# Regrouping the small matrix products of a gated linear recurrence: one visit across three heads, states and transposed outputs on their own

## The chip, the cores and the metric

The kernel runs on one core of one Trainium2 chip. Its engines work at the same time, each through its own instructions in order: TensorE (matrix products; PE in the profile, its weight loads PEld), VectorE (DVE), ScalarE (ACT), GpSimd (POOL), and SyncE (SP), which here only issues DMAs. TensorE writes its results to PSUM, eight banks of 128 x 512 floats; everything else lies in SBUF. The metric is device time of one execution in microseconds (us), the median of three.

## What is computed

One inference step of two layers over 272 prompt positions (16 learned ones ahead of 256) and 64 sample positions (8 sequences of 8), model width 2048. Layer 0 is a gated linear recurrence with 16 heads of 128, layer 1 a sliding-window attention. Only layer 0 is touched. For each head its projections are

```
q, fx, i, g = split(x @ w_in)            # four 128-wide columns per head
f = lb + (1 - lb) * sigmoid(fx);  k = 1 - f;  v = i
```

and in chunks of positions

```
b = cumsum(log f)
a[t, s] = sum_k q[t] * exp(b[t] - b[s]) * k[s]       # s <= t
o = (q * exp(b)) @ s0 + a @ v
s_new = exp(b_last) * s0 + (k * exp(b_last - b))^T @ v
```

After it, o is divided by its root mean square over the head, scaled, multiplied by silu(g), and goes through the output projection w_out, a residual and a LayerNorm. Outputs are the new states, the cache of layer 1 and the activations.

## The kernel before, in words

**Big products.** All projections run through `Stream`. A tile is one 128-wide output column block: 16 k blocks of 128, and for each k block three products of 128 x 128 weights with 128 x 336 activations (weights and activations are split in a high and a low part to keep float32 accuracy, L225 to L227). Weights come by DMA on SP into `raw` (L148), ACT casts the high part `whi` (L159), DVE subtracts to get `wlo` (L170), up to seven chunks of four k blocks ahead. A tile accumulates in a PSUM bank of the pool `pj` (three banks); at its end its `epi` function empties it. `kouter=True` runs several tiles side by side, chunk by chunk.

**Small work.** After the three products of each k block, `Stream.step` is called once. Generators in `st.side` hold everything else; a generator says by `yield n` that it wants its next piece n steps later, and at most two pieces run in a step. So the order on every engine is written out by these numbers, and no scheduler changes it. A piece issues its instructions at that place of all queues: its small products stand between two big ones on TensorE, its DVE work between two weight splits. A tile has 16 steps, a head's four tiles (in the order f, q, i, g) have 64.

**A head.** `epi_f` makes f and k on ACT and DVE. `epi_q` starts `head_chain`: three rounds of `update` (pairs, fours, eights) build scaled copies of k and q in `kx` and `qx` (a step of a tree of decay factors), then four `level` calls multiply them in 32-column products into the bank `lv_a` (52 steps into the head). `pick` copies the valid part by masks into `a32`; further updates (16, 32, 64) follow. When tile i is there, a second visit of TensorE makes the wide levels in `lv_b`, the outputs `po` of the head before, and the transposes `pk` and `pv`. From these the pieces `V`, `K`, `Ks`, `Vs` (ACT, DVE) and `vm` (POOL, L636) are made; `head_tail`, moved on by `adv`, multiplies the new states `psp` and `pss`, stores them, makes `po`, its squares and `ss` (L709 to L711), `osc` (L714), its transposes `pt` into the old `lv_b` bank (L720), and `og` with its split into `oh` and `ol`, the activations of the output projection.

So TensorE leaves the big products twice per head. The first visit, in tile g, holds levels 0 to 3 of head h, the states of h-1 and the transposes of `osc` of h-2. The second, at the start of the next head's tile f, holds the wide levels of h, the output of h-1, and `pk`, `pv` of h.

**End of the layer.** The output projection's tiles z0, z1, z2 run side by side, the rest one by one; `z_chain` takes each into a residual and running moments.

PSUM pools: `pj` three banks, `lv` two, `mm` three (all of `pk`, `pv`, `psp`, `pss`, `po`).

Of the kernel before, what the change touches and what calls it, by code (L numbers as in the profile page):

```python
# [21 lines left out]
F32 = mybir.dt.float32  # L22
# [217 lines left out]
def hybrid_trunk(tc, x_prompt, x_sample, state_hgrn, cache_k, cache_v, meta, w_in0, lb_logits, norm_w, w_out0,  # L240
# [7 lines left out]
    with es:  # L248
# [97 lines left out]
        for nm, w in (("f", 384), ("qp", 448), ("iT", 384), ("at", 3 * 132), ("a32", 96), ("sq0", 288),  # L346
                      ("sq1", 288), ("qi0", 177), ("qi1", 177), ("w64", 72)):
            one[nm] = hp1.tile([P, w], F32, tag=nm, name=nm)
            nc.gpsimd.memset(one[nm], 1.0 if nm == "w64" else 0.0)
        kx, qx = [], []  # L350
        for q in range(1, 4):
            for l, nm, w in ((kx, "kx", 384), (qx, "qx", 448)):
                l.append(hp1.tile([P, w], F32, tag=f"{nm}{q}", name=f"{nm}{q}"))
                nc.gpsimd.memset(l[-1], 0.0)
# [90 lines left out]
        def epi_g(h):  # L445
            def epi(ps):
                d = head_state(h)
                sg = hp.tile([P, T], F32, tag="sg", name=f"sg{h}")
                nc.scalar.activation(sg, ps, AF.Sigmoid)
                d["sg"] = sg  # L450
                s0 = hp.tile([P, 8, P], F32, tag="s0", name=f"s0_{h}")
                nc.sync.dma_start(s0, state_hgrn[0, :, h].rearrange("b k v -> k b v"))
                d["s0"] = s0

                def chain():
                    yield 2
                    nc.vector.tensor_tensor(sg, sg, ps, op=ALU.mult)  # L457
                    ready["g", h] = True
                st.spawn(chain())
            return epi  # L460
# [5 lines left out]
        def update(k, q, m, tot, n, k2=None, q2=None, nq=None):  # L466
# [5 lines left out]
            w = min(n, 448 - (m - 1)) // (2 * m) * 2 * m  # L472
# [4 lines left out]
            if q2 is not None and not nq:  # L477
                nc.scalar.copy(halves(q2, m - 1, m, w, True), halves(q, m - 1, m, w, True))
# [17 lines left out]
        tails = {}  # L496

        def adv(h):
            if h in tails:
                next(tails[h], None)  # L500

        def head_chain(h):
            d = head_state(h)
            kr, qp, a32, sq, qi = d["kr"], d["qp"], d["a32"], d["sq"], d["qi"]
            at = d["at"].rearrange("p (b w) -> p b w", b=3)
            kk = [kr] + kx
            qq = [qp] + qx

            def level(pl, o, li, wide=True):
                k, q = kk[min(li, 3)], qq[min(li, 3)]  # L510
                for blk in range(3):
                    for j in range(4 if blk < 2 else 3 if wide else 1):
                        c = blk * 128 + j * 32
                        nc.tensor.matmul(pl[32 * j:32 * j + 32, o + blk * 32:o + blk * 32 + 32], k[:, c:c + 32],
                                         q[:, c:c + 32], start=True, stop=True, tile_position=(0, 32 * j),
                                         skip_group_check=True)

            def pick(pl, o, li, wide=True):
                m0 = li * 96
                r = 96 if wide else 32  # L520
                nc.vector.copy_predicated(a32[:, 0:64], mk[:, m0:m0 + 64], pl[:, o:o + 64])
                nc.vector.copy_predicated(a32[0:r, 64:96], mk[0:r, m0 + 64:m0 + 96], pl[0:r, o + 64:o + 96])

            tot = {1: d["f"]}
            yield 3
            for li in range(3):
                m = 1 << li
                update(kk[li], qq[li], m, tot[m], 352, kk[li + 1], qq[li + 1])
                tot[2 * m] = total(h, m, tot[m], 352)
                yield 4  # L530

            k8, q8 = kk[3], qq[3]
            fs = hp.tile([P, 8], F32, tag="fs", name=f"fs{h}")
            t8 = tot[8]
            nc.gpsimd.tensor_copy(fs, t8[:, 36:44])
            w64 = d["w64"]
            nc.gpsimd.tensor_copy(w64[:, 0:64].rearrange("p (b t) -> p b t", t=8)[:, :, 7], fs)

            for s in range(3):
                n = 3 if s < 2 else 2  # L540
                nc.gpsimd.tensor_tensor(sq[:, 0:96 * n].rearrange("p (j w) -> p j w", w=96)[:, :, 40 * s:40 * s + 8],
                                        q8[:, 288:288 + 24 * n].rearrange("p (j w) -> p j w", w=24)[:, :, 8 * s:8 * s + 8],
                                        w64[:, 0:24 * n].rearrange("p (j w) -> p j w", w=24)[:, :, 8 * s:8 * s + 8],
                                        op=ALU.mult)
            yield 4

            pa = lv.tile([P, 512], F32, tag="lv", name=f"lv{h}_a")
            for li in range(4):
                level(pa, 96 * li, li)
            adv(h - 1)  # L550
            adv(h - 2)
            yield 1
            update(k8, q8, 8, t8, 272)
            tot[16] = hp.tile([P, 17], F32, tag="tot16", name=f"tot{h}_16")
            t8v = t8[:, 0:34].rearrange("p (b two) -> p b two", two=2)
            nc.vector.tensor_tensor(tot[16], t8v[:, :, 0], t8v[:, :, 1], op=ALU.mult)
            for li in range(4):
                pick(pa, 96 * li, li)
            adv(h - 1)
            yield 2  # L560
            t16 = tot[16][:, 16:17]
            update(k8, q8, 16, tot[16], 256, kk[1], qq[1])
            tot[32] = total(h, 16, tot[16], 256)
            nc.vector.tensor_scalar(qq[1][:, 271:272], q8[:, 271:272], t16, None, op0=ALU.mult)
            yield 3
            adv(h - 2)
            update(kk[1], qq[1], 32, tot[32], 256, kk[2], qq[2])
            nc.scalar.copy(qi[:, 144:161], qq[1][:, 255:272])
            t64 = total(h, 32, tot[32], 256)
            t128 = hp.tile([P, 2], F32, tag="t128", name=f"t128_{h}")  # L570
            nc.vector.tensor_tensor(t128[:, 0:1], t64[:, 2:3], t64[:, 3:4], op=ALU.mult)
            yield 3
            adv(h - 1)
            k64 = kk[2]
            nc.vector.tensor_tensor(halves(kr, 0, 64, 256), halves(k64, 0, 64, 256),
                                    t64.rearrange("p (b two) -> p b two", two=2)[:, :, 1:2].to_broadcast([P, 2, 64]),
                                    op=ALU.mult)
            nc.scalar.copy(halves(kr, 0, 64, 256, True), halves(k64, 0, 64, 256, True))
            nc.vector.tensor_scalar(qi[:, 64:128], qq[2][:, 191:255], t64[:, 2:3], None, op0=ALU.mult)
            nc.scalar.copy(qi[:, 0:64], qq[2][:, 127:191])  # L580
            yield 5
            while ("i", h) not in ready:
                yield 0

            pb = lv.tile([P, 512], F32, tag="lv", name=f"lv{h}_b")
            d["pb"] = pb
            level(pb, 0, 4, wide=False)
# [11 lines left out]
            adv(h - 1)  # L599
            iT = d["iT"]  # L600
            pk = pm(f"pk{h}")
            for j in range(3):
                nc.tensor.transpose(pk[:, j * P:(j + 1) * P], (kr if j < 2 else k8)[:, j * P:(j + 1) * P], ident)
            pv = pm(f"pv{h}")
            for j in range(3):
                nc.tensor.transpose(pv[:, j * P:(j + 1) * P], iT[:, j * P:(j + 1) * P], ident)
            yield 1
            pick(pb, 0, 4, wide=False)
            for a in range(2):
                nc.scalar.copy(at[64 * a:64 * a + 32, 0:2, 64 * a + 32:64 * a + 64],  # L610
                               pb[64 * a:64 * a + 32, 96:160].rearrange("p (b w) -> p b w", b=2))
            nc.scalar.copy(at[0:64, 0:2, 64:128], pb[0:64, 160:288].rearrange("p (b w) -> p b w", b=2))
            for blk in range(3):
                o = 1 if blk < 2 else 0
                nc.vector.copy_predicated(
                    at[:, blk, o:o + 128].rearrange("p (j w) -> p j w", w=32),
                    mk[:, 480 + blk * 128:608 + blk * 128].rearrange("p (j w) -> p j w", w=32),
                    a32[:, blk * 32:blk * 32 + 32].unsqueeze(1).to_broadcast([P, 4, 32]))
            V = hp1.tile([P, 3, P], F32, tag="V", name=f"V{h}")
            K = hp1.tile([P, 2, P], F32, tag="K", name=f"K{h}")  # L620
# [27 lines left out]
            for w, us in ((1, (h - 1,)), (3, (h - 1,)), (6, (h,)), (2, (h - 1, h)), (1, (h - 1, h)), (4, (h,)), (3, (h,)),  # L648
                          (2, (h,)), (4, (h,)), (1, (h,))):
                yield w  # L650
                for u in us:
                    adv(u)
# [849 lines left out]
```

## Time and profile before

| | |
|---|---|
| median of three | 1157.65 us (1157.64 to 1157.77) |
| the profiled execution | 1157.71 us, its span 1155.7 us |
| mean granted TensorE clock | 0.997 |
| TensorE busy | 1141.5 us, 10151 products |
| DVE, ACT, POOL busy | 795.2, 620.2, 238.9 us |
| one head (f to the next f) | 35.2 us |

The span runs from the first instruction to the last of one execution under the profiler; the time of that execution is some 2 us longer. Rows of a timeline are: start in us, duration in us, engine, source line, operation, output<-inputs, shape, count, and in brackets the idle time ahead of it with what ended it. Products on TensorE overlap one another, so one that takes 0.31 us does not mean that the next starts 0.31 us later. In rows of the stretches (a:b) follow the length, each engine's busy time with its number of instructions, the granted clock, the DMA share and GB/s.

### The profile page before, as it was taken

How to read it: one execution, taken by the hardware profiler on the slowest of the kernel's cores; microseconds unless marked ns; L12 is line 12 of the kernel's file. 1: busy time of each engine (PE TensorE's matmuls, PEld its weight loads, DVE VectorE, ACT ScalarE, POOL GpSimd, SP SyncE). 2: the span in 40 equal slices, each digit the busy share in tenths (PEclk: the TensorE clock that was granted, in tenths of full speed). 3: DMA queues.
4: the chain of work that ended last, by engine and by line, in shares of the span. 5: the costliest groups of instructions: out<-in, count | busy, mean ns of one | idle time of the engine just before them, and what ended most of it. 6: DMA issues, size and time to landing. Idle time of an engine off the chain costs nothing.

```text
span 1155.7 us, 26360 instructions
## 1 busy us (share of the span) xinstructions
PE 1141.5 (99%) x10151; PEld 1104.2 (96%) x10151; DVE 795.2 (69%) x2094; ACT 620.2 (54%) x1771; POOL 238.9 (21%) x343
## 2 busy tenths in 40 slices
PE   9999999999999999999999999999999999999996
PEld 8999999999999999999999999999999999999995
DVE  4766566666576566666678777577877767787656
ACT  5664555545555545555445445566566655555540
POOL 2131221212211212212134332100000011145510
PEclk9999999999999999999999999999999999999998
DMA  9644565455554545654555555743443535545572
GB/s 262 188 141 132 164 185 146 134 144 156 164 167 135 145 135 164 182 148 134 145 153 144 147 146 153 216 125 106 120 118 97 141 101 167 146 133 160 153 213 91
DMA packets 322877, 173.39 MB, mean 150 GB/s; under 512 B 19104, under 2 KB 317536, under 8 KB 322720
## 3 DMA queue, kind: packets, MB, share of 16 engines
q1 hardware_dynamic: 320656, 166.98, 51.4%
q0 software_dynamic: 1344, 4.20, 1.4%
q8 instruction: 80, 1.31, 0.5%
q10 hardware_dynamic: 752, 0.52, 0.1%
q14 instruction: 45, 0.37, 0.1%
HBM read 158.88 MB, written 14.42 MB: 150 GB/s over the span
## 4 chain that ended last, share of the span: by engine, by line
PE 95%; DVE 2%; DMA 1%; ACT 1%; issue 0%; SPq 0%; POOL 0%; DVEq 0%
PE pj_g L225 7%; PE pj_g L226 7%; PE pj_g L227 7%; PE pj_q L225 7%; PE pj_q L226 6%; PE pj_q L227 6%; PE pj_f L225 3%; PE pj_i L225 3%; PE pj_z L225 3%; PE pj_f L226 3%; PE pj_i L227 3%; PE pj_z L227 3%; PE pj_i L226 3%; PE pj_f L227 3%; PE pj_z L226 3%; PE pj_y L225 2%
## 5 line engine op out<-in xcount | busy, mean ns | idle before, releaser
L225 PE MATMUL pj_q<-xh,wlo_q 128*128 128x336 f32 (+1 forms) x512 | 163.3, 319 | 0.0
L225 PE MATMUL pj_g<-xh,wlo_g 128*128 128x336 f32 (+1 forms) x512 | 163.1, 318 | 0.0
L226 PE MATMUL pj_g<-xl,whi_g 128*128 128x336 f32 (+1 forms) x512 | 160.6, 314 | 0.0
L226 PE MATMUL pj_q<-xl,whi_q 128*128 128x336 f32 (+1 forms) x512 | 160.6, 314 | 0.0
L227 PE MATMUL pj_g<-xh,whi_g 128*128 128x336 f32 (+1 forms) x512 | 160.4, 313 | 0.0
L227 PE MATMUL pj_q<-xh,whi_q 128*128 128x336 f32 (+1 forms) x512 | 160.2, 313 | 0.0
L225 PEld LDWEIGHTS pj_q<-xh,wlo_q 128*128 128x128 f32 x512 | 96.6, 189 | 2.5 <-issue 1.4
L225 PEld LDWEIGHTS pj_g<-xh,wlo_g 128*128 128x128 f32 x512 | 96.6, 189 | 0.7 <-issue 0.3
L226 PEld LDWEIGHTS pj_g<-xl,whi_g 128*128 128x128 f32 x512 | 96.9, 189 | 0.0
L226 PEld LDWEIGHTS pj_q<-xl,whi_q 128*128 128x128 f32 x512 | 96.8, 189 | 0.0
L227 PEld LDWEIGHTS pj_q<-xh,whi_q 128*128 128x128 f32 x512 | 96.6, 189 | 0.0
L227 PEld LDWEIGHTS pj_g<-xh,whi_g 128*128 128x128 f32 x512 | 96.5, 189 | 0.0
L170 DVE TENSOR_TENSOR wlo_g<-raw_g,whi_g 128x512 fp32r<-128x512 f32 x128 | 91.6, 750 | 0.0
L159 ACT CAST whi_g<-raw_g 128x512 fp32r<-128x512 f32 x128 | 76.5, 622 | 22.4 <-DMA raw_g<-in_hgrn_w_in_dram 16.7
L636 POOL TENSOR_TENSOR vm<-Vs,cst 96x512 fp32r<-96x512 f32 x32 | 33.8, 1055 | 252.4 <-DVE Vs L633 251.3
L170 DVE TENSOR_TENSOR wlo_q<-raw_q,whi_q 128x512 fp32r<-128x512 f32 x128 | 85.1, 684 | 1.0 <-ACT whi_q L159 1.0
L225 PE MATMUL pj_f<-xh,wlo_f 128*128 128x336 f32 x256 | 82.7, 323 | 0.0
L225 PE MATMUL pj_z<-oh,wlo_z 128*128 128x336 f32 x256 | 81.4, 318 | 1.3 <-DVE sg L457 1.3
L225 PE MATMUL pj_i<-xh,wlo_i 128*128 128x336 f32 x256 | 81.5, 318 | 0.0
L227 PE MATMUL pj_z<-oh,whi_z 128*128 128x336 f32 x256 | 81.2, 317 | 0.0
L226 PE MATMUL pj_f<-xl,whi_f 128*128 128x336 f32 x256 | 81.1, 317 | 0.0
L226 PE MATMUL pj_z<-ol,whi_z 128*128 128x336 f32 x256 | 81.0, 316 | 0.0
(404 smaller groups left out, 3213.7 us busy)
## 6 DMA issues: line engine op xcount, KB each, us to landing
raw_z<-in_hgrn_w_out_dram SPq DMA_DIRECT2D x32, 512.0 KB
raw_q<-in_swa_w_in_dram SPq DMA_DIRECT2D x32, 512.0 KB
raw_g<-in_swa_w_in_dram SPq DMA_DIRECT2D x32, 512.0 KB
raw_f<-in_hgrn_w_in_dram SPq DMA_DIRECT2D x30, 512.0 KB
raw_q<-in_hgrn_w_in_dram SPq DMA_DIRECT2D x30, 512.0 KB
raw_i<-in_hgrn_w_in_dram SPq DMA_DIRECT2D x30, 512.0 KB
raw_g<-in_hgrn_w_in_dram SPq DMA_DIRECT2D x30, 512.0 KB
raw_y<-in_swa_w_out_dram SPq DMA_DIRECT2D x24, 512.0 KB
```

The costliest lines, as they stand in the source:

```text
L159: e.nc.scalar.copy(hi, t["raw", kc])
L170: e.nc.vector.tensor_tensor(lo, t.pop(("raw", kc)), hi.bitcast(F32), op=ALU.subtract)
L225: nc.tensor.matmul(ps, lo[:, kk, :], xh, start=first, stop=False)
L226: nc.tensor.matmul(ps, hi[:, kk, :], xl, start=False, stop=False)
L227: nc.tensor.matmul(ps, hi[:, kk, :], xh, start=False, stop=last)
L636: nc.gpsimd.tensor_tensor(vm[0:96, 4 * u:4 * u + 4, :], Vs[:, u, :].bitcast(F32).unsqueeze(1).to_broadcast([96, 4, P]), cst[0:96, 0:4].uns ...
```

## The change

The two visits become one per head, `visit0(h)`, which comes 52 steps into the head: levels 0 to 3 of head h, wide levels of h-1, output of h-2, and the transposes `pk` and `pv` of h-1. It runs when `due(h)` says that its inputs have been issued. Behind it, `attended(h-1)` fills `at`, `states(h-1)` makes V, K, Ks, Vs and `vm` and inserts the products `psp` and `pss` by themselves, and `normed(h-2)` makes squares, `ss` and `osc` and inserts the three transposes `pt` by themselves, in a `mm` bank. To let three heads be under way, `kx` and `qx` get two sets, by the head's parity, `sg` three buffers; `ns` takes the place of `vm`, and the squares' unused output goes to `osc`. The load of the old state `s0` is issued later, 56 steps into the head. Tiles run in the order f, q, g, i, and the group of z tiles side by side has four, the fourth in an `lv` bank.

```diff
-        kx, qx = [], []
...
+        kx, qx = ([], []), ([], [])
+        for par in range(2):
...
-                sg = hp.tile([P, T], F32, tag="sg", name=f"sg{h}")
+                sg = hp.tile([P, T], F32, tag="sg", name=f"sg{h}", bufs=3)
...
-        tails = {}
...
+        def visit0(h, pa=None):
+            if pa is not None:
+                for li in range(4):
+                    level(hd[h], pa, 96 * li, li)
+            if 1 <= h <= H:
+                wide_levels(h - 1)
+            if h >= 2:
+                output(h - 2)
+            if 1 <= h <= H:
+                d = hd[h - 1]
+                d["pk"], d["pv"] = pm(f"pk{h - 1}"), pm(f"pv{h - 1}")
...
+            if h >= 2:
+                st.spawn(normed(h - 2), 1)
+
+        def due(h):
+
+            return all(n < 0 or n >= H or (nm, n) in ready
+                       for nm, n in (("i", h - 1), ("b", h - 1), ("at", h - 2), ("S", h - 2)))
...
+        def head_chain(h):
...
+            yield 3
+            for li in range(3):
+                m = 1 << li
+                update(kk[li], qq[li], m, tot[m], 352, kk[li + 1], qq[li + 1])
+                tot[2 * m] = total(h, m, tot[m], 352)
+                yield 4
...
+            nc.gpsimd.tensor_copy(fs, t8[:, 36:44])
+            yield 4
+            while not due(h):
+                yield 0
+            pa = lv.tile([P, 512], F32, tag="lv", name=f"lv{h}_a")
+            visit0(h, pa)
+            yield 1
+            if h:
+                attended(h - 1)
+                st.spawn(states(h - 1), 2)
+                yield 1
+            for li in range(4):
+                pick(d, pa, 96 * li, li)
+            yield 2
+            update(k8, q8, 8, t8, 272)
...
+            s0 = d["s0"] = hp.tile([P, 8, P], F32, tag="s0", name=f"s0_{h}")
+            nc.sync.dma_start(s0, state_hgrn[0, :, h].rearrange("b k v -> k b v"))
...
+            yield 2
...
+            update(k8, q8, 16, tot[16], 256, kk[1], qq[1])
...
+            yield 3
+            update(kk[1], qq[1], 32, tot[32], 256, kk[2], qq[2])
...
+            yield 3
...
+            ready["b", h] = True
+            if h < H - 1:
+                return
+            yield 2
+            while not due(H):
+                yield 0
+            yield 2
+            visit0(H)
+            yield 1
+            attended(h)
+            st.spawn(states(h), 1)
+            while not due(H + 1):
+                yield 0
+            yield 3
+            visit0(H + 1)
+
+        def states(h):
...
+            quick = h >= H - 2
...
+            nc.scalar.copy(V.rearrange("p j v -> p (j v)"), pv[:, 0:384])
+            nc.scalar.copy(K.rearrange("p j v -> p (j v)"), pk[:, 0:256])
...
+            yield 2 if quick else 4
...
+            vm = hp1.tile([P, 8, P], F32R, tag="vm", name=f"vm{h}")
+            for u in range(2):
+                r = slice(32 + 32 * u, 64 + 32 * u)
+                for t, src, again, low in ((Ks, pk, 64, 32), (Vs, pv, 32, 64)):
+                    nc.scalar.copy(t[0:32, u, :], src[r, 256:384])
+                    nc.scalar.copy(t[again:again + 32, u, :], src[r, 256:384])
+                    nc.vector.tensor_tensor(t[low:low + 32, u, :], src[r, 256:384], t[0:32, u, :].bitcast(F32),
+                                            op=ALU.subtract)
+                nc.gpsimd.tensor_tensor(vm[0:96, 4 * u:4 * u + 4, :],
...
+                yield (8 if quick else 9) if u else (3 if quick else 4)
...
+            yield 1
+            S = d["S"] = hp1.tile([P, 2, P], F32, tag="S", name=f"S{h}")
...
+            ns = hp1.tile([P, 8, P], F32, tag="vm", name=f"ns{h}")
...
+            yield 3 if quick else 6
...
+        def normed(h):
...
+                nc.scalar.activation(osc[:, j, :], po[:, j * P:(j + 1) * P], AF.Square, accum_out=ss[:, j:j + 1])
...
-            yield
+            yield 4
             nc.vector.tensor_tensor(osc, po[:, 0:384].rearrange("p (j v) -> p j v", j=3),
                                     ss[:, 0:3].unsqueeze(2).to_broadcast([P, 3, P]), op=ALU.mult)
-            yield
-
-            pt = hd[h + 1]["pb"] if h < H - 1 else pm(f"pt{h}")
+            yield 3
+
+            pt = pm(f"pt{h}")
             for j in range(3):
                 nc.tensor.transpose(pt[:, j * P:(j + 1) * P], osc[:, j, :], ident)
-            yield
+            yield 1
...
-        first = [tiles[nm, 0] for nm in "fqig"]
+        first = [tiles[nm, 0] for nm in "fqgi"]
...
-            yield 1 + 6 * j if j < 3 else 1
+            yield 1 + 4 * j if j < 4 else 1
...
-        st.add(zt[:3], kouter=True)
-        st.add(zt[3:])
+        zt[3]["bank"] = lv, "lv"
+        st.add(zt[:4], kouter=True)
+        st.add(zt[4:])
```

Each generator's pieces still run in the step that its numbers give, counted from the step in which it was started.

298 lines of the change are left out of this document (120 added, 178 removed).

## The prediction

> **What bounds the kernel now.** I read the page's parts 1 and 4 first, then the stretches (one head, from the first product of tile f to the next f), then the timeline of each engine.
>
> ```profile
> PE 1141.5 (99%) x10151; PEld 1104.2 (96%) x10151; DVE 795.2 (69%) x2094; ACT 620.2 (54%) x1771; POOL 238.9 (21%) x343
> ...
> PE 95%; DVE 2%; DMA 1%; ACT 1%; issue 0%; SPq 0%; POOL 0%; DVEq 0%
> ...
> 323.59:358.78 35.19, 35.19 (x367) 34.40 (x366) 22.35 (x71) 18.66 (x58) 6.83 (x9) 1.00 0.54 153
> ```
>
> TensorE ends everything: 95% of the chain, and 35.19 of a head's 35.19 us, at full clock. DVE (22.35) and ACT (18.66) have room on average. So time is won where TensorE does less, and lost wherever a DVE, ACT or POOL result is late at a place in TensorE's order.
>
> The unit is the big 128x336 product. The first and the 97th of a stretch without small products:
>
> ```profile
> 299.74 0.32 PE L225 MATMUL pj_q<-xh,wlo_q 128*128 128x336 f32 x1
> ...
> 314.51 0.32 PE L225 MATMUL pj_g<-xh,wlo_g 128*128 128x336 f32 x1
> ```
>
> 14.77 us for 96 starts: 0.154 us each. A step of the Stream is three of them, 0.46 us; a head has 64 steps. What an insertion costs is the time from the big product ahead of it to the second one behind it, less two starts (0.31). I take the second because the first one behind is drawn out:
>
> ```profile
> 315.29 0.31 PE L227 MATMUL pj_g<-xh,whi_g 128*128 128x336 f32 x1
> ...
> 315.74 0.82 PE L514 MATMUL lv_a<-qx,kx 128*32 128x32 f32 x65
> ...
> 318.21 0.32 PE L226 MATMUL pj_g<-xl,whi_g 128*128 128x336 f32 x1
> ...
> 324.36 0.31 PE L227 MATMUL pj_f<-xh,whi_f 128*128 128x336 f32 x1
> ...
> 326.65 0.39 PE L704 MATMUL po<-V,at 128*128 128x128 f32 x2
> ...
> 327.69 0.31 PE L226 MATMUL pj_f<-xl,whi_f 128*128 128x336 f32 x1
> ```
>
> First visit (levels 0 to 3, states, transposed outputs): 318.21-315.29-0.31 = 2.61. Second (wide levels, output, the transposes pk and pv): 327.69-324.36-0.31 = 3.02. Together 5.63 per head.
>
> **The change on TensorE.** No product is added or dropped; they are regrouped into one visit (levels of head h, wide levels of h-1, output of h-2, pk/pv of h-1), one insertion for the states, one for the three transposes pt. The old trace holds each alone: head 0's levels, head 15's states, head 14's transposes.
>
> ```profile
> 48.03 0.31 PE L227 MATMUL pj_f<-xh,whi_f 128*128 128x336 f32 x1
> 48.27 0.36 PE L514 MATMUL lv_a<-qp,kr 128*32 128x32 f32 x19
> ...
> 49.65 0.32 PE L227 MATMUL pj_f<-xh,whi_f 128*128 128x336 f32 x1
> ...
> 580.42 0.32 PE L227 MATMUL pj_z<-oh,whi_z 128*128 128x336 f32 x1
> 580.57 0.83 PE L660 MATMUL psp<-V,K 128*128 128x128 f32 x6
> 581.16 0.71 PE L664 MATMUL pss<-vm,Ks 96*128 96x512 f32 x2
> ...
> 581.86 0.31 PE L226 MATMUL pj_z<-ol,whi_z 128*128 128x336 f32 x1
> ...
> 582.47 0.33 PE L227 MATMUL pj_z<-oh,whi_z 128*128 128x336 f32 x1
> 582.63 0.49 PE L720 MATMUL lv_b<-ident,osc 128*128 128x128 f32 x3
> ...
> 583.12 0.32 PE L226 MATMUL pj_z<-ol,whi_z 128*128 128x336 f32 x1
> ```
>
> Levels alone: 49.65-48.03 less three starts (this row is the third product behind) = 1.16. States alone: 1.44-0.31 = 1.13. Transposes alone: 0.65-0.31 = 0.34. Sum 2.63 against 2.61 in the old visit: giving the last two insertions of their own costs 0.02. Levels ahead of other 32-column products cost their inside alone:
>
> ```profile
> L514 PE MATMUL lv_a<-qx,kx 128*32 128x32 f32 x1056 | 14.0, 198 | 0.0
> ```
>
> They start 0.24 behind the big product (48.27-48.03; so at 315.53 in the first visit) and end at 315.74+0.82 = 316.56; without the last one's own 0.20 that is 0.83, with the step to the next 0.85. The rest of the 1.16 is entering and leaving the 32-column form. So joining saves 1.16-0.85 = **0.31 us**, and it happens 15 times (visits of heads 1 to 15): **-4.7 us**. Bounds: 0 (the change of form is paid anyway) and 0.5.
>
> At the end of the layer:
>
> ```profile
> 576.57 0.32 PE L227 MATMUL pj_z<-oh,whi_z 128*128 128x336 f32 x1
> 578.15 0.42 PE L225 MATMUL pj_z<-oh,wlo_z 128*128 128x336 f32 x1 [1.26 <-DVE sg L457]
> ```
>
> The third z tile waits for the PSUM bank of g15, whose product with its sigmoid (L457) sits on DVE behind the second visit. With order f, q, g, i the bank before it is i15's, emptied by two ACT copies, and g15 is done 13 steps sooner. The start is 1.58 instead of 0.154 late: **-1.4 us**. The fourth z tile in the outer-k group moves the first need of head 15's output from step 40 of z to step 52; by the yields that output is issued at step 37, so nothing is late there. The six more memsets on POOL run before anything needs POOL; the state load moved to step 56 stands on SP behind weight loads that run a tile ahead: both 0, and about 1 us once if that cover goes.
>
> **What the new order asks of DVE, ACT and POOL.** I count yields. The visit runs at step 52 of a head. Step 53: mask and copies of `at`, then the squares of `normed`; 54: eight masked picks and a weight split; 56: update 8; 57: `osc`; 58: update 16 and a split; 59: first half of Ks/Vs and `vm`; 60: pt on TensorE; 61: update 32, then `og` and its split; 62: weight split; 63: second half of Ks/Vs and `vm`; 72: the states on TensorE. Before, `osc` had about 45 steps until pt; now it has 3, and `vm` has 9. Each engine works in order, so everything on that list up to `osc` delays pt, and a waiting pt holds all big products behind it.
>
> ```profile
> 327.07 0.42 ACT L610 COPY at<-lv_b 32x64 f32<-32x64 f32 x2 [2.33 <-PE po L704]
> ...
> 327.73 0.48 ACT L621 COPY V<-pv 128x384 f32<-128x384 f32 x1
> ...
> 331.47 0.28 ACT L709 ACTIVATE junk<-po 128x128 f32<-128x128 f32 x1
> ...
> 316.58 0.30 DVE L475 TENSOR_TENSOR kx<-kx,tot 128x136 f32<-128x136 f32 x1 [5.34 <-PE lv_a L514]
> ...
> 317.09 0.22 DVE L521 COPY_PREDICATED a<-mk,lv_a 128x64 f32<-128x64 uint8 x1
> ...
> 318.11 0.34 DVE L669 SCALAR_TENSOR_TENSOR S<-S,t,psp 128x128 f32<-128x128 f32 x1
> ...
> 318.75 0.68 DVE L170 TENSOR_TENSOR wlo_f<-raw_f,whi_f 128x512 fp32r<-128x512 f32 x1
> 319.35 0.28 DVE L475 TENSOR_TENSOR kx<-kx,tot 128x128 f32<-128x128 f32 x1
> ...
> 319.96 0.88 DVE L725 SCALAR_TENSOR_TENSOR og<-lv_b,tv,sg 128x255 f32<-128x255 f32 x4
> ...
> 321.99 0.28 DVE L475 TENSOR_TENSOR kx<-kx,tot 128x128 f32<-128x128 f32 x1
> ...
> 332.67 0.17 DVE L710 TENSOR_SCALAR ss<-ss 128x3 f32<-128x3 f32 x1 [1.00 <-ACT junk L709]
> ...
> 334.18 0.56 DVE L714 TENSOR_TENSOR osc<-po,ss 128x384 f32<-128x384 f32 x1 [0.74 <-POOL ss L711]
> ```
>
> Clock 0 is the end of the output products (L704, 326.65+0.39 = 327.04). ACT starts the `at` copies at 0.03 and needs 0.66 (327.07 to 327.73); squares until DVE's `ss`: 1.20 (331.47 to 332.67), so 1.89. Then DVE: `ss` 0.1, picks 1.02 (317.09 to 318.11), split 0.60 (318.75 to 319.35), update 8 0.51 (316.58 to 317.09), `osc` 0.56: ready at 4.68. POOL's power of `ss` (1.5 from `ss` to `osc` in those rows) ends inside this. TensorE gets there sooner: 327.69-327.04 to the second big product, then 22 starts to the 24th, with which pt's weights are due (one start ahead): 0.65+22x0.154 = 4.04. **Wait at pt: 0.64, taken as 0.7** with the small POOL products beside update 8; bounds 0.2 and 1.1. It falls on the 14 heads 0 to 13 and, by a similar list, head 14: 15x0.7 = **+10.5 us**.
>
> Next the states. DVE goes on at 4.6: update 16 0.61 (319.35 to 319.96), split 0.60, two halves of Ks/Vs, then update 32, `og` with its split 2.03 (319.96 to 321.99), split 0.60, two more halves. Here POOL meets DVE:
>
> ```profile
> L636 POOL TENSOR_TENSOR vm<-Vs,cst 96x512 fp32r<-96x512 f32 x32 | 33.8, 1055 | 252.4 <-DVE Vs L633 251.3
> ...
> L633 DVE TENSOR_TENSOR Vs<-pv,Vs 32x128 fp32r<-32x128 f32 x32 | 9.2, 287 | 8.6 <-ACT Vs L632 8.6
> ...
> 580.51 2.98 DVE L170 TENSOR_TENSOR wlo_z<-raw_z,whi_z 128x512 fp32r<-128x512 f32 x2
> ...
> 581.05 1.90 POOL L675 TENSOR_TENSOR ns<-s,fs 128x1024 f32<-128x1024 f32 x1 [1.05 <-DMA s<-in_state_hgrn_dram]
> ```
>
> Two splits that take 1.3 elsewhere took 2.98, the second ending 0.54 behind POOL's product: DVE stood still until POOL was done. The Trainium skill, "SBUF — State Buffer", section "Who interferes with whom", states the same as a rule: a VectorE instruction with two SBUF inputs and a GpSimd instruction that reads SBUF shut each other out for a whole instruction. The trace agrees by the 2.98; this rule speaks against the change, for the old order ran `vm` beside DVE products that read PSUM, and the new one beside update 32.
>
> So: 4.6+0.61+0.60+2x0.28 = 6.4, `vm` takes POOL; update 32 0.7 plus 1.06 blocked = 8.1; +2.03+0.60+0.56 = 11.3; the second `vm` behind one DVE product (0.28), 1.06: ready at 12.6. TensorE: pt at 4.04, plus 0.34 and 36 starts = 9.92 to psp, 0.74 more to the weights of the second pss, plus the 0.7 lost at pt: 11.4. **Wait 1.2, taken as 1.1** because no row shows so small an update being blocked; bounds 0 (unblocked, ready at 11.3) and 1.5. It falls on the states of heads 1 to 13 (head 0's visit has no `normed`; heads 14 and 15 have fewer lists in the way): 13x1.1 = **+14.3 us**. Behind it DVE has 44 steps to catch up before the next visit; 22.4 busy plus some 4 blocked fit a head.
>
> **Sum.** -4.7-1.4+10.5+14.3 = +18.7. The profiled execution took 1157.71 us (span 1155.7, and 2.0 around it); the median of three is 1157.65. So **1176.4 us**.
>
> **Rivals.** (1) Faster: DVE and ACT keep up, and only the regrouping shows: 1157.7-6.1 = 1151.6. For it: 31% of DVE is free; against: the list ahead of `osc` is 4.7 long and must shrink below 4.04. It decides from there on. Chance 0.17. (2) Small waits only (0.4 at pt, none at the states) that eat the gain: 1157.7-6.1+6 = 1157.6; 0.12. (3) pt waits, POOL does not block update 32 (its DVE products are 0.3 each, the split that stood still 0.68): 1157.7-6.1+10.5 = 1162.1, up to 1165; 0.22. (4) The delay goes on: splits fall so far behind that SP's weight loads, which wait for the same buffers, are late too; the states wait 1.5 and a tile start waits once per head for 0.3: 1186; 0.06. (5) The change doesn't do what it says: joining saves nothing since the form must be left anyway; the forecast loses its 4.7: 1181; 0.05. My forecast, 1168 to 1180: 0.38.
>
> About 0.2% (2.3 us) is what a measurement can tell from no change. Faster by more: case 1 and a little of 2, 0.19. Within: the rest of 2, 0.11. Slower: 0.70. The range 1154 to 1183 leaves out case 1 and the far end of 4.
>
> **What would show it.** Right: one insertion of 162 small products per head costing 3.9, one of 8, one of 3; TensorE idle 0.5 to 1 ahead of pt with DVE `osc` as releaser, and ahead of pss with POOL `vm`; update 32 lengthened to above 1 us beside `vm`; no wait in z. Wrong: pt following within 0.17 of the big product ahead of it (case 1), pss starting 0.59 behind psp (case 3), or a visit costing 4.2 (case 5). A list executed in another order than I count by the yields would undo both waits.

## The result, and the profile after

The changed kernel takes **1179.59 us** (median of four, 1179.14 to 1179.75), the kernel before 1157.71 beside it: 1.84 % slower, ratio 1.0184 with an interval of 1.0171 to 1.0196. The forecast was 1176.4. Line numbers are those of the new kernel from here on: psp L705, pss L709, pt L745, `vm` L699, the squares L735, `osc` L739, updates L473 and L477. Where a kernel with one visit per head instead of two loses 22 us is read from the views in this order. First the page, its parts 1 and 4:

```profile
PE 1144.6 (97%) x10151; PEld 1103.4 (94%) x10151; DVE 837.9 (71%) x2094; ACT 613.3 (52%) x1771; POOL 254.4 (22%) x349
...
PE 75%; DVE 8%; issue 6%; ACT 4%; DMA 3%; POOL 3%; SPq 0%; POOLq 0%; ACTq 0%; DVEq 0%
```

TensorE is still busy 97 % of the time, but it held 95 % of the chain before and holds 75 % now: other engines end last in places. DVE shows 43 us more busy time for exactly as many instructions (2094). Instructions that got longer without any more work are standing still for something. The stretch of one head, from visit to visit:

```profile
283.41:319.86 36.45, 35.41 (x367) 34.40 (x365) 25.21 (x70) 18.25 (x58) 7.88 (x9) 1.00 0.53 147
```

36.45 us against 35.19, at the same full clock (1.00), with TensorE idle for 1.04 and DVE 2.9 longer. Who ended TensorE's idle times is in the list of its waits (total, times, longest):

```profile
PE pss L709 <- POOL vm L699: 12.7, 13, 1.0
PE po L557 <- DVE sp L717: 2.0, 1, 2.0
PE pt L745 <- DVE osc L739: 1.1, 1, 1.1
...
PE pj_z L225 <- DVE wlo_z L170: 1.0, 1, 1.0
PE pss L709 <- DVE og L752: 1.0, 1, 1.0
```

The first row is the regular loss, thirteen heads; the other four happen once each, at the end of the layer. The timeline of TensorE in that same head shows the three insertions, each with the big product ahead of it and the second one behind:

```profile
283.32 0.31 PE L227 MATMUL pj_i<-xh,whi_i 128*128 128x336 f32 x1
...
287.49 0.31 PE L226 MATMUL pj_i<-xl,whi_i 128*128 128x336 f32 x1
...
290.88 0.32 PE L227 MATMUL pj_i<-xh,whi_i 128*128 128x336 f32 x1
291.26 0.52 PE L745 MATMUL pt<-ident,osc 128*128 128x128 f32 x3
...
291.77 0.32 PE L226 MATMUL pj_i<-xl,whi_i 128*128 128x336 f32 x1
...
297.00 0.31 PE L227 MATMUL pj_f<-xh,whi_f 128*128 128x336 f32 x1
...
297.81 0.47 PE L709 MATMUL pss<-vm,Ks 96*128 96x512 f32 x1
299.25 0.50 PE L709 MATMUL pss<-vm,Ks 96*128 96x512 f32 x1 [0.97 <-POOL vm L699]
...
299.75 0.32 PE L226 MATMUL pj_f<-xl,whi_f 128*128 128x336 f32 x1
```

Counted as in the prediction (less two starts, 0.31): the visit 3.86, pt 0.58, the states 2.44, together 6.88 where the two old visits cost 5.63. That is the 1.25 us by which a head got longer. Alone, in the old trace, the transposes cost 0.34 and the states 1.13, so **0.24 of pt and 1.31 of the states are waiting**. The wait at pt isn't in the list of waits: it is a gap of 0.38 between two starts, where 0.15 is normal, too small to be put down as idle. Only the sum of starts shows it.

The other engines beside it:

```profile
287.46 0.27 ACT L735 ACTIVATE osc<-po 128x128 f32<-128x128 f32 x1
...
287.72 0.26 ACT L735 ACTIVATE osc<-po 128x128 f32<-128x128 f32 x1
...
288.36 0.17 DVE L736 TENSOR_SCALAR ss<-ss 128x3 f32<-128x3 f32 x1
...
290.57 0.54 DVE L739 TENSOR_TENSOR osc<-po,ss 128x384 f32<-128x384 f32 x1
...
293.05 1.14 POOL L699 TENSOR_TENSOR vm<-Vs,cst 96x512 fp32r<-96x512 f32 x1 [1.66 <-DVE Vs L697]
293.21 1.13 DVE L477 TENSOR_TENSOR qx<-qx,tot 128x128 f32<-128x128 f32 x1
...
298.06 1.14 POOL L699 TENSOR_TENSOR vm<-Vs,cst 96x512 fp32r<-96x512 f32 x1 [3.87 <-DVE Vs L697]
```

The half of update 32 on `qx` (L477) starts 0.16 behind POOL's first `vm` and ends 0.15 behind its end: 1.13 us for a product that takes 0.3 elsewhere. The second `vm` is done at 299.20, and the second pss starts then.

Last, the timeline at the end of the layer, one row for each loss there:

```profile
589.29 0.48 PE L709 MATMUL pss<-vm,Ks 96*128 96x512 f32 x1 [1.04 <-DVE og L752]
589.85 2.10 POOL L721 TENSOR_TENSOR ns<-s,fs 128x1024 f32<-128x1024 f32 x1 [2.20 <-PE pss L709]
590.11 2.39 DVE L170 TENSOR_TENSOR wlo_z<-raw_z,whi_z 128x512 fp32r<-128x512 f32 x1
594.25 0.27 PE L557 MATMUL po<-S,qi 128*32 128x128 f32 x1 [1.97 <-DVE sp L717]
596.83 0.62 ACT L159 CAST whi_z<-raw_z 128x512 fp32r<-128x512 f32 x1 [5.12 <-DMA raw_z<-in_hgrn_w_out_dram]
601.71 0.52 PE L745 MATMUL pt<-ident,osc 128*128 128x128 f32 x3 [1.13 <-DVE osc L739]
643.76 0.42 PE L225 MATMUL pj_z<-oh,wlo_z 128*128 128x336 f32 x1 [1.05 <-DVE wlo_z L170]
```

A weight split stands still beside POOL's `ns` (2.39 instead of 0.68). Behind it on DVE is `S`, which the output of head 14 waits for, and ACT, whose `at` copies and squares that head's pt needs, waits 5.1 us for a weight load. From the big product ahead to the first one behind, the states of head 14 take 2.59 us (1.29 without a wait), the visit with its output 5.30 (3.09 for the same products before), its pt 1.72 (0.40); the seventh z tile starts 1.2 late. Together 6.0 us.

**The balance.** 15 visits at 0.30 saved: -4.5; the old wait of the third z tile, which is gone: -1.4; 14x0.24 at pt: +3.4; 13x1.31 at the states: +17.0; end of the layer: +6.0. Sum 20.5; the spans differ by 21.9 (1177.6 against 1155.7). Of the 1.4 that is left, 0.7 lies behind the last product of the z tiles, in a part of the program that neither kernel changes. The rest is about what the visits of heads 2, 3, 10 and 11 cost above the others (4.01, 4.12, 4.28 and 3.94 for 3.84, together 1.0). Every other kernel with joined visits has some such heads, mostly 2, 3 and 9 to 12; the kernel before and c1_levels_apart have none. Their cause isn't shown.

### The profile page after: what moved, and what is told of

It reads as the page before. It is cut to its first block, busy times and chain, and to the rows that moved or that the text cites. A ratio compares the mean times of both kernels' runs of the same rounds, so it can differ in the third digit from the quotient of the medians.

```text
span 1177.6 us, 26336 instructions
## 1 busy us (share of the span) xinstructions
PE 1144.6 (97%) x10151; PEld 1103.4 (94%) x10151; DVE 837.9 (71%) x2094; ACT 613.3 (52%) x1771; POOL 254.4 (22%) x349
## 3 DMA queue, kind: packets, MB, share of 16 engines
q8 instruction: 80, 1.31, 0.5%
## 4 chain that ended last, share of the span: by engine, by line
PE 75%; DVE 8%; issue 6%; ACT 4%; DMA 3%; POOL 3%; SPq 0%; POOLq 0%; ACTq 0%; DVEq 0%
PE pj_g L225 7%; PE pj_g L226 7%; PE pj_g L227 6%; PE pj_q L225 6%; PE pj_q L226 6%; PE pj_q L227 6%; POOL vm L699 3%; PE pj_z L225 2%; PE pj_z L227 2%; PE pj_z L226 2%; PE pj_f L225 2%; PE pj_f L226 2%; PE pj_f L227 2%; PE pj_y L225 2%; PE pj_y L227 2%
## 5 line engine op out<-in xcount | busy, mean ns | idle before, releaser
L170 DVE TENSOR_TENSOR wlo_g<-raw_g,whi_g 128x512 fp32r<-128x512 f32 x128 | 105.0, 845 | 0.0
L227 PE MATMUL pj_i<-xh,whi_i 128*128 128x336 f32 x256 | 81.0, 316 | 0.0
L226 PE MATMUL pj_i<-xl,whi_i 128*128 128x336 f32 x256 | 81.0, 316 | 0.0
```

The costliest lines, as they stand in the source:

```text
L170: e.nc.vector.tensor_tensor(lo, t.pop(("raw", kc)), hi.bitcast(F32), op=ALU.subtract)
L226: nc.tensor.matmul(ps, hi[:, kk, :], xl, start=False, stop=False)
L227: nc.tensor.matmul(ps, hi[:, kk, :], xh, start=False, stop=last)
```

## The experiments

Each kernel ran beside the kernel before on the same chip. They ran in three groups (e, c and d), each on another chip; the kernel before took 1158.1 to 1158.2 us in each of them and 1157.7 beside the changed kernel, so a difference below 0.5 us between two groups says nothing.

| kernel | us | ratio to before (interval) |
|---|---|---|
| e1_states_later | 1162.47 | 1.0035 (1.0023 to 1.0047) |
| e2_og_first | 1166.74 | 1.0074 (1.0062 to 1.0087) |
| e3_squares_one_tile | 1183.80 | 1.0220 (1.0206 to 1.0234) |
| e4_last_ns_later | 1183.82 | 1.0221 (1.0207 to 1.0235) |
| c1_levels_apart | 1168.21 | 1.0084 (1.0070 to 1.0098) |
| c2_pt_later | 1159.49 | 1.0009 (1.0000 to 1.0017) |
| c3_last_ns_on_act | 1157.84 | 0.9995 (0.9986 to 1.0004) |
| c4_old_tile_order | 1163.16 | 1.0042 (1.0028 to 1.0056) |
| d2_z_spread | 1157.34 | 0.9990 (0.9981 to 0.9999) |
| d1_best | 1154.91 | 0.9971 (0.9959 to 0.9982) |

### Is the wait at the states a matter of a fixed time, or of engines at their limit?

```diff
-                yield (8 if quick else 9) if u else (3 if quick else 4)
+                yield (8 if quick else 13) if u else (3 if quick else 4)
```

> The changed kernel with one number changed: the states (psp, pss) are inserted 13 steps behind the second vm instead of 9; the last two heads stay as they are. Theory (the second vm is ready a fixed time behind the visit, and TensorE comes 1.3 us too early for it in heads 1 to 13): four steps are 1.85 us, more than the wait, so the idle time of TensorE ahead of the second pss of those heads goes and the states cost 1.29 instead of 2.59 us: 1179.6-13x1.30 = 1162.7 us. Rival (the engines run at their limit through the head, and a wait taken away here comes back at the next pt, the next visit or a tile start): within 2 us of 1179.6.

Measured 1162.47, 17.1 us less than the changed kernel, where 16.9 was expected. TensorE in the same head (first row: the product ahead; last: the second behind):

```profile
292.13 0.32 PE L227 MATMUL pj_f<-xh,whi_f 128*128 128x336 f32 x1
...
292.88 0.71 PE L709 MATMUL pss<-vm,Ks 96*128 96x512 f32 x2
...
293.58 0.32 PE L226 MATMUL pj_f<-xl,whi_f 128*128 128x336 f32 x1
```

The two pss stand in one row now, back to back, and the insertion costs 1.14: the price of the states alone. Nothing came back elsewhere. So most of the loss is one number in the hand-written order: the states come 1.3 us before POOL can be ready, and four steps of the Stream cover it.

### What makes `vm` late?

```diff
             nc.vector.tensor_scalar(qq[1][:, 271:272], q8[:, 271:272], t16, None, op0=ALU.mult)
-            yield 3
+            yield 4
             update(kk[1], qq[1], 32, tot[32], 256, kk[2], qq[2])
...
-            yield 3
+            yield 2
             k64 = kk[2]
```

> The changed kernel with update 32 moved one step later in every head (and what follows it kept in place), so that og, whose inputs lie in PSUM, is issued ahead of it and DVE works on og and not on update 32 while POOL makes the first vm. Theory (POOL's vm and DVE's product of two SBUF tiles exclude each other, which delays the whole list up to the second vm): the qx half of update 32 falls from 1.13 to about 0.3 us, the second vm is ready some 0.8 us sooner, the wait ahead of the second pss falls from 1.30 to about 0.5 in heads 1 to 13: 1179.6-13x0.84 = 1168.7 us. Rival (it is only the length of the list and the step numbers, and nothing excludes anything): the same work in the same steps, within 2 us of 1179.6, and the qx half stays at 1.1.

Measured 1166.74 us: 12.9 less, where 10.9 was expected. DVE, POOL and TensorE in one head:

```profile
252.67 1.04 POOL L699 TENSOR_TENSOR vm<-Vs,cst 96x512 fp32r<-96x512 f32 x1 [1.66 <-DVE Vs L697]
...
254.86 0.28 DVE L477 TENSOR_TENSOR qx<-qx,tot 128x128 f32<-128x128 f32 x1
...
256.62 0.32 PE L227 MATMUL pj_f<-xh,whi_f 128*128 128x336 f32 x1
...
258.42 0.32 PE L226 MATMUL pj_f<-xl,whi_f 128*128 128x336 f32 x1
```

The same instructions with two neighbours exchanged: the `qx` half takes 0.28 instead of 1.13, the states 1.49 instead of 2.44. `og`, which now runs beside the first `vm`, isn't lengthened: its four products take 0.89 us in both kernels. The Trainium skill, "SBUF — State Buffer", section "Who interferes with whom", says that a VectorE instruction with two inputs in SBUF and a GpSimd instruction that reads SBUF exclude each other, and that one with at most one SBUF input, outside the modes that take two ports, doesn't contend. The trace agrees, with 1.13 for the product of two SBUF tiles and an unchanged 0.89 for `og`, whose `pt` lies in PSUM. So the exclusion is real and worth 0.95 us per head here; it is a cause of the late `vm`, not all of it, since 0.36 of wait stays.

### Why did pt wait for 0.24 and not 0.7?

```diff
-                nc.scalar.activation(osc[:, j, :], po[:, j * P:(j + 1) * P], AF.Square, accum_out=ss[:, j:j + 1])
+                nc.scalar.activation(osc[:, 0, :], po[:, j * P:(j + 1) * P], AF.Square, accum_out=ss[:, j:j + 1])
```

> The changed kernel with the unused output of all three squares in one place (the first third of osc), as the kernel before had it in junk. Theory (the wait at pt came out at 0.26 instead of 0.7 because the three squares follow each other by 0.255 us when each has an output of its own, and by 0.40 when they share one): ss comes 0.3 us later behind the first square, osc and pt with it, the insertion of pt costs 0.66+0.3 to 0.4 us in 14 heads: 1179.6+14x0.35 = 1184.5 us, if the time lost there isn't won back at the states (then 1179.6 and a wait at pss that is shorter by as much). Rival (DVE's list sets pt, and the squares are done long before they count): the distance of the squares doesn't matter, pt stays at 0.66 and the time at 1179.6.

Measured 1183.80, where 1184.5 was expected. ACT, DVE and TensorE:

```profile
289.08 0.27 ACT L735 ACTIVATE osc<-po 128x128 f32<-128x128 f32 x1
...
289.48 0.28 ACT L735 ACTIVATE osc<-po 128x128 f32<-128x128 f32 x1
...
290.28 0.17 DVE L736 TENSOR_SCALAR ss<-ss 128x3 f32<-128x3 f32 x1 [0.35 <-ACT osc L735]
...
292.50 0.32 PE L227 MATMUL pj_i<-xh,whi_i 128*128 128x336 f32 x1
293.19 0.52 PE L745 MATMUL pt<-ident,osc 128*128 128x128 f32 x3 [0.37 <-DVE osc L739]
...
293.70 0.32 PE L226 MATMUL pj_i<-xl,whi_i 128*128 128x336 f32 x1
```

The squares follow each other by 0.40 us when they write one place, and by 0.26 (287.46, 287.72) when each has its own; `ss` comes 1.20 instead of 0.90 behind the first. pt costs 0.89, its wait 0.55 instead of 0.24: 14x0.31 = 4.3, and the kernel got 4.2 us slower. The states still cost as much as before (2.59 from the product ahead to the first behind, in both), so the two waits add up and don't pay for each other.

### Does joining the levels to the visit save anything?

```diff
-            visit0(h, pa)
+            for li in range(4):
+                level(d, pa, 96 * li, li)
+            yield 1
+            visit0(h)
             yield 1
```

> The changed kernel with the states 4 steps later (as in e1_states_later, 1162.5 us), and with levels 0 to 3 of a head as an insertion of their own at step 52 and the rest of the visit one step behind them. Theory (a stretch of 32-column products costs 0.31 us to enter and leave, which joining saves 15 times): levels alone 1.16, the rest 3.91-0.85 = 3.06, together 4.22 instead of 3.91: 1162.5+15x0.31 = 1167.1 us. Rival (the change of form inside a visit is paid anyway, and joining saves nothing): the two insertions add up to 3.91 and the time is 1162.5.

Measured 1168.21, 5.7 above e1_states_later. For each of the two insertions, the product ahead and the second behind:

```profile
278.63 0.31 PE L227 MATMUL pj_i<-xh,whi_i 128*128 128x336 f32 x1
...
280.09 0.31 PE L226 MATMUL pj_i<-xl,whi_i 128*128 128x336 f32 x1
280.25 0.32 PE L227 MATMUL pj_i<-xh,whi_i 128*128 128x336 f32 x1
...
283.57 0.32 PE L226 MATMUL pj_i<-xl,whi_i 128*128 128x336 f32 x1
```

Levels 1.15 and the rest 3.01: 4.16 against 3.86 joined. A stretch of 32-column products costs **0.30 us** to enter and leave, 15 times 4.5 us. The other 1.2 us above e1 went to pt, 0.05 longer in each head here, and to the pt of head 14.

### A step more for pt

```diff
                                     ss[:, 0:3].unsqueeze(2).to_broadcast([P, 3, P]), op=ALU.mult)
-            yield 3
+            yield 4
```

> As e1_states_later (1162.5 us), with the transposes pt 4 steps behind osc instead of 3. Theory (pt comes 0.26 us too early in 14 heads): a step is 0.46 us, the insertion costs 0.40 instead of 0.67 us: 1162.5-14x0.27 = 1158.7 us. Rival (0.40 isn't to be had in the middle of a head, where ident and osc are read beside DVE and ACT): 0.67 stays, 1162.5.

Measured 1159.49, 3.0 less than e1_states_later; 3.8 was expected. The insertion costs 0.40 in every head, from the product ahead to the first behind, as forecast. At the end of the layer, pt of head 14 lost its wait as well (0.41 for 1.83), but the visit ahead of it costs 6.71 for 5.30. The wait for `sp` in it is the same 1.97; behind it the granted clock of TensorE is 0.50 for some 3 us of this profile, where the changed kernel keeps 1.00:

```profile
575.00:576.00 1.00, 1.00 (x5) 1.00 (x6) 0.62 (x3) 0.00 (x0) 0.00 (x0) 0.50 1.12 326
```

So there the loss only changed its place, and what lowered the clock isn't shown.

### What is late at the end of the layer?

```diff
+            if h == H - 2:
+                yield 4
             ns = hp1.tile([P, 8, P], F32, tag="vm", name=f"ns{h}")
```

> The changed kernel with POOL's product ns of head 14 alone issued 4 steps later than S and sp of that head; all other heads as they are. Theory for the end of the layer (ns keeps DVE's weight split out for 2.4 us; that makes S late for the output of head 14, where the visit costs 5.30 instead of 3.09 us, and frees a weight buffer late, so that the next load lands late and ACT waits 5.1 us for it, which the pt of head 14 waits for): the split takes 0.7 us, the visit costs about 3.5, ACT's wait gets 1.7 us shorter: 1179.6-1.8-1.7 = 1176.1 us. Rival (the loads are late since four tiles side by side share four buffers, and S since DVE's list is long): the visit and the pt of head 14 stay within 0.3 us of 5.30 and 1.73, and the time at 1179.6.

A miss: 1183.82 us, 4.2 more and not 3.5 less. POOL and DVE at the place in question:

```profile
589.44 2.11 POOL L723 TENSOR_TENSOR ns<-s,fs 128x1024 f32<-128x1024 f32 x1 [2.19 <-PE pss L709]
589.71 2.39 DVE L170 TENSOR_TENSOR wlo_z<-raw_z,whi_z 128x512 fp32r<-128x512 f32 x1
```

`ns` starts 0.55 behind the second pss (588.89), as it did before the edit (589.85 and 589.29), though it is issued four steps later. A step number sets the place in an engine's queue. POOL's queue was empty, so `ns` ran as soon as its inputs and its buffer were free, and the split, which starts 0.27 behind it (not ahead of it, as the next expectation has it), stood still as before. What did come later were its additions on DVE, and with them the bank that `pk` needs: a wait of 3.3 us. In this profile, too, the granted clock is 0.50 there, from 595 to 604 us. The edit didn't test the theory. This one does:

```diff
+            if h == H - 2:
+                for b in range(8):
+                    nc.scalar.activation(ns[:, b, :], s0[:, b, :], AF.Copy, scale=fs[:, b:b + 1])
+            else:
                 nc.gpsimd.tensor_tensor(ns, s0, fs.unsqueeze(2).to_broadcast([P, 8, P]), op=ALU.mult)
```

> As c2_pt_later, with ns of head 14 alone made by ACT (eight copies scaled by fs) instead of POOL. e4_last_ns_later didn't settle the question, since POOL started ns at the same place (0.16 us behind the start of DVE's split there): its buffer came free then and nothing stood ahead of it in POOL's queue, and only its additions came later. Theory as there (POOL's ns keeps DVE's split out for 1.7 us, so S is late and the next weight load too): the split beside it takes 0.7 us, the visit with the output of head 14 costs about 3.6 instead of 5.30 us, and the pt of head 14 some 0.6 instead of 1.4 to 1.8: 2.5 to 3 us below c2_pt_later, 1155.9 us if that one is 1158.7. Rival (four tiles side by side on four buffers make the loads late, and DVE's list makes S late): the same as c2_pt_later within 1 us.

Measured 1157.84, 1.65 below c2_pt_later where 2.5 to 3 was expected. The same place, without `ns` on POOL:

```profile
570.47 0.68 DVE L170 TENSOR_TENSOR wlo_z<-raw_z,whi_z 128x512 fp32r<-128x512 f32 x1
...
572.98 0.27 PE L557 MATMUL po<-S,qi 128*32 128x128 f32 x1 [0.34 <-DVE sp L717]
...
575.60 0.62 ACT L159 CAST whi_z<-raw_z 128x512 fp32r<-128x512 f32 x1 [1.20 <-DMA raw_z<-in_hgrn_w_out_dram]
```

The split takes 0.68 instead of 2.39, the output waits 0.34 for `sp` instead of 1.97, and ACT's wait for the load is 1.20 instead of 5.30 in c2_pt_later. ACT spent 2.45 of that difference on `ns` itself; counted from the second pss, the load lands 1.8 us sooner. So the theory holds: one POOL product made S late by standing in DVE's way, and the load by holding the buffer that it goes to. The gain was overestimated, since part of it is waited for again. TensorE leaves the visit 2.9 us sooner than in c2_pt_later (3.82 for 6.71, some 1.4 of it by the clock, which is 1.00 here), but `osc` is ready only 1.8 us sooner: pt of head 14 costs 1.16 for 0.41, and the states of head 15 cost 1.77 for 1.30. Together that is 1.7 us less, as measured. What still makes the load late by 1.20 isn't shown; the four buffers that the rival names weren't tested.

### The tile order and the z tiles

```diff
-        first = [tiles[nm, 0] for nm in "fqgi"]
+        first = [tiles[nm, 0] for nm in "fqig"]
...
-        st.add([tiles[nm, h] for h in range(1, H) for nm in "fqgi"])
+        st.add([tiles[nm, h] for h in range(1, H) for nm in "fqig"])
```

> As e1_states_later (1162.5 us), with the tiles of a head in the order f, q, i, g of the kernel before. Theory of the prediction (the order f, q, g, i takes away the 1.4 us that the third z tile waited for the bank of g15, whose product with its sigmoid stands in DVE's queue): the wait ahead of the third z tile comes back with 1 to 1.4 us: 1163.5 to 1163.9 us. Rival (what stood ahead of that product in DVE's queue was the old second visit, and it went with it): no wait there, 1162.5.

With i ahead of g, the values `iT` of head h are written before the visit transposes those of h-1 into `pv`, so in this kernel `pv`, and what follows from it, is made from the values of h; no instruction is added or dropped. Measured 1163.16: 0.7 above e1, less than the spread of either. The list of waits has no z tile that waits for a bank, so the wait of 1.26 us is gone in both orders. But the rival's cause isn't shown either. This is the product with g's sigmoid, first in the kernel before, then here:

```profile
577.59 0.50 DVE L457 TENSOR_TENSOR sg<-sg,pj_g 128x336 f32<-128x336 f32 x1
...
577.36 0.49 DVE L456 TENSOR_TENSOR sg<-sg,pj_g 128x336 f32<-128x336 f32 x1
```

It ends 8.1 us behind the first z product in the kernel before (at 570.00), and 8.5 us behind it here (569.31): it came no sooner. TensorE asks for the bank later. Before, the third z tile was due 6.7 us behind the first z product. Here the states of head 14 (2.58) and the visit of heads 14 and 15 (6.95) stand between the two, and it starts 12.9 us behind (582.23). In the changed kernel, with the new order, the bank is the one that i15's copies empty; it is free 5.2 us behind the first z product (590.51 less 585.33), and the third tile starts 11.3 us behind. Without the visit it would be due some 6.1 us behind, an estimate from the second tile's start (589.61) and twelve starts more. So in the changed kernel either is enough, the order or the visit ahead of the tile.

```diff
-            yield 1 + 4 * j if j < 4 else 1
+            yield 1 + 5 * j if j < 4 else 5 if j == 4 else 1
```

> As c3_last_ns_on_act (1157.8 us), with the work behind the z tiles side by side put 5 steps apart instead of 4 (and that of the fifth tile 4 steps later). Theory (the wait of 1.04 us ahead of the fifth z tile, which the kernel before doesn't have, comes from that work: 2.7 us of DVE per tile every 1.85 us, so that the weight splits come late): at 2.3 us per tile and with less of it ahead of the split the wait goes, 1.2 us less: 1156.6. Rival (the split is late because its load is late): the wait stays, 1157.8.

Measured 1157.34, 0.5 less (1.2 was expected). The wait stands ahead of the seventh z tile, by the count of products ahead of it (six tiles of 48), and not ahead of the fifth. Its row:

```profile
PE pj_z L225 <- DVE wlo_z L170: 0.3, 1, 0.3
```

0.3 for 1.0: the spacing of the z work is the cause of most of it. The rest of the expected gain is within the spread of the two kernels, and whether it was won isn't settled.

```diff
-                yield (8 if quick else 13) if u else (3 if quick else 4)
+                yield (11 if quick else 13) if u else (3 if quick else 4)
```

> As d2_z_spread, with the states of heads 14 and 15 inserted 11 steps behind the second vm instead of 8. Theory (the second pss of head 14 waits 1.3 us for the bank that og of head 12 empties, that of head 15 about 0.4 us for vm; three steps are 1.4 us): both waits go, 1156.6-1.3-0.4 = 1154.9 us, 0.3 % below the kernel before. Rival (what is won ahead of the output of head 14 is waited for behind it, since S and the loads come three steps later): no gain against d2_z_spread, 1156.6.

Measured 1154.91, 2.4 less than d2, where 1.7 was expected: both waits at pss are gone (the states of head 14 take 1.45 and those of head 15 1.29, for 2.87 and 1.77). The bank that head 14's waited for is emptied by `og` of head 13, the last one ahead of it, not of head 12. A little was paid back. The third z tile now starts ahead of the visit, and it waits for the bank of i15:

```profile
569.92 0.42 PE L225 MATMUL pj_z<-oh,wlo_z 128*128 128x336 f32 x1 [0.34 <-ACT iT L443]
```

It is the one kernel that beats the kernel before clearly, by 0.29 % (0.18 to 0.41); the interval of d2_z_spread ends just below 1.

## Why the prediction was right, point by point

**The regrouping, -4.7: right.** 0.30 per head measured, in the trace (5.63 for 3.86+0.34+1.13) and by undoing it (c1), for 0.31.

**The z tile's wait, -1.4: right in size; the cause named is one of two.** The bank is i15's now and free in time, as forecast. But the old order has no wait either (c4), because the states and the visit now stand ahead of the third z tile and TensorE asks for the bank later. The prediction saw the order and not the visit. Where the visit comes behind the start of that tile (d1_best), the new order leaves a wait of 0.34.

**The wait at pt, 0.7 x 15 = +10.5: mechanism right, size too large.** It was 0.24 x 14 = 3.4 (the fifteenth, of head 14, is in the loss at the end of the layer). The step that failed is "squares until DVE's `ss`: 1.20", which was taken from rows where all three squares write `junk`. The change gives each its own third of `osc`, and 1.20 became 0.90; a shared place in the new kernel brings back 1.20 and a wait of 0.55 (e3). Of the 0.15 between that and 0.7, 0.06 is rounding up. The edit of the outputs stood in the diff and was passed over, since it moves no work.

**The wait at the second pss, 1.1 x 13 = +14.3: right, slightly small.** It was 1.31 x 13 = 17.0. Update 32 was lengthened to 1.13 beside `vm`, as the list had it, and the exclusion is what e2 took away. On the prediction's clock the `vm` was ready at 12.4 (299.20 less 286.84, the end of the output products) for 12.6, and TensorE came to psp at 10.3 (297.15) for 10.6: both a little sooner, so the error at pt hardly showed here. The two waits aren't set off against each other: with pt 0.31 longer, the states cost the same (e3).

**"Nothing is late" in z, and only short lists for heads 14 and 15, 0: wrong.** This cost 6.0 us. The prediction counted by the yields when head 15's output is issued, and it is issued in time. It did not follow the blocking that it had itself found to the last heads, where `ns` meets a weight split, `S` is needed at once, and the buffer behind that split is the next load's. The z edit, costed at nothing, makes a burst on DVE (most of 1.2 of the 6.0, by d2_z_spread).

So the forecast of 1176.4 is 3.2 low with errors that partly cancel: pt 7.1 too much, the states 2.7 too little, the end 6.0 and the rest 1.6 too little. In the chances by direction, those of the cases add up to 0.10 for within and 0.71 for slower, for the 0.11 and 0.70 written.

**Rivals:** (1), keeping up, didn't happen, but it is near: d1_best, a handful of numbers of the order and one product moved to another engine away from the changed kernel, takes 1154.9 where the rival had 1151.6. (2), small waits only, fell by the thirteen waits ahead of the second pss. (3), no blocking by POOL, fell by the row of 1.13. (5), nothing saved, fell by c1. (4), delays that reach the weight loads, happened once, at the end of the layer, and not in every head.

## What to carry to other kernels

Where the order is written out by hand, joining small products pays by what the change of form costs (0.30 us a time here), and is lost at once where the regrouped results are asked for some steps too soon: price the list behind every insertion against the steps that it is given, and give it one more. Keep VectorE products of two SBUF tiles away from a GpSimd instruction that reads SBUF (1.13 us for 0.28 here), and put work that reads PSUM beside it instead (0.89 in both places); follow that conflict into the last rounds of a loop, where nothing absorbs it. A later place in an idle engine's queue delays nothing: the instruction starts when its inputs and its buffer are free (0.55 us behind the second pss, issued early or late).

## What the runs showed of the hardware that was not expected

Three ScalarE squares of 128x128 with an accumulated sum start 0.40 us apart when they write the same unused output and 0.26 apart when each writes its own, with the instruction itself at 0.26 to 0.28 in both: sharing a scratch output costs 0.3 us for three (e3). Whether the second square waits for the write of the first by the program's own order or inside the engine isn't shown.

Also blocked beside the second `vm` is a VectorE instruction with one SBUF tile and a scalar for each partition (L657), in the changed kernel:

```profile
298.22 1.03 DVE L657 TENSOR_SCALAR qi<-qx,tot 128x64 f32<-128x64 f32 x1
```

It takes 1.03 in heads 1 to 14 of that kernel, and 0.24 to 0.25 where POOL is idle (heads 0 and 15, and at 571.27 us in c3_last_ns_on_act). The Trainium skill, "SBUF — State Buffer", section "Who interferes with whom", lists this form among those that can take the shared ports, if their operands allow a faster mode; this row agrees, with 1.03 for 0.25.

In four of the profiles (e2, e4, c2, c4) the granted clock of TensorE falls to 0.50 behind the wait for `sp` at the end of the layer, for 3 to 4 us, and for some 10 us in e4, where the wait for the bank of `pk` follows. That wait is 1.97 us in two of them and 2.37 to 2.38 in the others. In four more (the changed kernel, e1, e3, c1) it is 1.96 to 1.98 us and the clock stays at 1.00. What decides isn't shown.
